# The first adaLN vectors by TensorE in quarters of the columns, and the first products in two parts along K

## The chip, the cores and the metric

The kernel runs on one core of one Trainium2 chip. The metric is the device time of the whole kernel in microseconds (us), taken as the median of several runs.

## What is computed

Two layers of a decoder trunk on one sequence of 512 tokens, 1024 features, all float32. Only the beginning of layer 0 matters here: a conditioning vector `c` gives six vectors of 1024 (shift, scale and gate of two sub-layers), the normed input is scaled and shifted by them, and one wide projection follows, of whose columns `dt`, `B` and `C` are taken first.

```
cs  = silu(c)                                   # 1024
mod = cs @ ada_w[0] + ada_b[0]                  # 1024 x 6144
sh1, sc1, g1, sh2, sc2, g2 = split(mod, 6)
h   = rms_norm(x, norm_mix_g[0]) * (1 + sc1) + sh1
z, xbc, dt_raw, q, k, v = split(h @ w_in)       # xbc: x, then B and C of 4 groups
xbc = silu(causal_depthwise_conv(xbc))          # 4 taps
dt  = softplus(dt_raw + dt_bias)
y   = ssd_chunked(x, dt, A, B, C)               # 4 groups of heads, chunks of 128 tokens
...                                             # gate by z, attention, output projection, FFN, layer 1
```

## The kernel before

Features lie on the partitions, tokens along the free axis: a product's output is 128 features by 512 tokens, one bank of PSUM. Each fp32 weight slab is split by ScalarE (ACT) and one other engine into a rounded part `hi` and a rest `lo` (`slab`), the activations likewise (`hh`, `hl` of `h`), and a product of K = 1024 is 24 matmuls: for each of 8 pieces of K `hi` and `lo` against `hh`, then 8 times `hi` against `hl` (`products`, L206, L207, L209). VectorE (DVE) makes most rests; for wdt, wbc, wx of group 0 it is GpSimd (POOL), by `SL`.

The head of the program, in the order of the code: SP loads two slabs of 1 MB for each of four column blocks of `ada_w` that the first norm needs (`ada_load`; blocks 8 and 12 are the scale, 0 and 4 the shift, 512 columns each) and `x`. `ada_wide` makes a block on DVE: one multiply and seven multiply-adds of 128 x 512 by the entries of `cs` (L159, L161), then four transposes by TensorE (PE) and a reduce. `x` is squared and scaled by its norm on ACT (`xn`), transposed by PE both as it is (`xT`, copied by ACT) and normed (`turned(xn, ...)`); ACT multiplies by the gain (`n_g`) and adds the shift (`hh`), DVE makes `hl`. Then the product of dt, then B and C of group 0 (`ssm_inputs`), whose banks go through `conv_tile` (ACT, three DVE rows that read the bank, tanh, one DVE row), the softplus of dt in a row of small DVE operations, the four products of x, then four of z.

In each of four groups, `ssm_group` then works through four chunks: `ar` is loaded from a copy of the cumulated decay in HBM, minus `acs` on POOL, minimum on DVE, exp on ACT, times `cb` on DVE, and multiplied by `xdt` on PE (`pd`). The two buffers of `ar` serve first for two tables of the attention bias (`hot`, `bv`), which PE turns into three pieces (`bv0` to `bv2`); the chunk loads can start when these are done with them.

PSUM tags `pj`, `A`, `B`, `C` have two banks each. The order of instructions on each engine is not the code's: a scheduler that simulates the engines sets it when the program is built. `tc.issue_after` holds a few rows back: the rests `hl` behind the last block of adaLN (`LATE`), the product of dt behind its last transpose (`GDT`), the loads of small vectors and of wdt behind the last adaLN load (`AFT`). adaLN columns 16 to 47 are made later, on POOL (`ada_pool`, tiles `adap`), beside the group's work.

## Time and profile before

| | |
|---|---|
| median of 3 runs | 1886.85 us (1884.89 to 1888.67) |
| the profiled execution | 1896.6 us, span 1894.8 us |
| PE busy | 1770.6 us, 93% of the span |
| DVE, ACT, POOL busy | 1150.2, 761.5, 564.4 us |
| mean granted clock of PE | 0.968 |

Busy time of PE is not work at its peak: matmuls are pipelined and a row's length holds its tail, so the distance from one start to the next is what a matmul costs in a stream. The granted clock is 1.0 at 2.4 GHz and 0.5 at 1.2 GHz; in the first 20 us the profile prints 1.00 where it has no record. Rows of the timeline merge like instructions in a row (x4) and name in brackets how long the engine stood before them and what ended that.

### The profile page before, as it was taken

To read this page: it belongs to the slowest core of one execution; us is meant where nothing else is said; L and a number is where in the kernel's file an instruction comes from. 1 tells how busy PE (TensorE), PEld (TensorE's weight loads), DVE (VectorE), ACT (ScalarE), POOL (GpSimd) and SP (SyncE) were. 2 spreads that over 40 slices of the span, in tenths; PEclk is the share of its full clock that TensorE was granted. 3 is DMA by queue.
4 is the path that set the end of the run, shared out by engine and by line. 5 is a ranking of instruction groups with operands and counts; after the bars stand their busy time and mean duration, and the time that the engine had idled before them with its cause. 6 is when DMAs were issued, how large, how long until landed. Compare 5 with 4: busy or idle time off the path is not lost.

```text
span 1894.8 us, 24381 instructions
## 1 busy us (share of the span) xinstructions
PE 1770.6 (93%) x9277; PEld 1475.4 (78%) x9277; DVE 1150.2 (61%) x2168; ACT 761.5 (40%) x1476; POOL 564.4 (30%) x486
## 2 busy tenths in 40 slices
PE   5897979999999999989999999979899899999998
PEld 3675767777788778768888888878799888888887
DVE  7859687755655565458774673386896643333336
ACT  6333333335445454245222222346775432122225
POOL 1437786412443340003000000056993400000001
PEclk8998989999999999999999999989999899999999
DMA  8354545634544543434655553242211423322223
GB/s 302 99 138 141 149 129 138 158 99 140 141 122 139 135 133 105 130 102 134 222 182 173 186 192 93 92 149 62 73 45 35 132 79 105 97 89 95 83 94 129
DMA packets 225779, 238.94 MB, mean 126 GB/s; under 512 B 11755, under 2 KB 195885, under 8 KB 225662
## 3 DMA queue, kind: packets, MB, share of 16 engines
q1 hardware_dynamic: 214525, 195.44, 34.4%
q0 software_dynamic: 11136, 41.95, 6.7%
q8 instruction: 73, 1.20, 0.3%
q14 instruction: 45, 0.36, 0.1%
HBM read 228.72 MB, written 8.64 MB: 125 GB/s over the span
## 4 chain that ended last, share of the span: by engine, by line
PE 73%; DVE 11%; DMA 6%; ACT 4%; issue 3%; POOL 2%; SPq 0%; DVEq 0%; POOLq 0%; ACTq 0%
PE fd L206 4%; PE fd L209 4%; PE fd L207 4%; PE fg L207 4%; PE fg L206 4%; PE fu L206 4%; PE fu L207 4%; PE fu L209 4%; PE fg L209 4%; PE cps L1012 2%; DMA ar<-a_dram 1%; PE s L716 1%; PE z L206 1%; PE z L207 1%; PE qq L206 1%
## 5 line engine op out<-in xcount | busy, mean ns | idle before, releaser
L248 POOL TENSOR_TENSOR n_acc<-n_acc,n_q 128x256 f32<-128x256 f32 x32 | 27.6, 864 | 545.6 <-ACT n_q L244 545.5
L194 DVE TENSOR_TENSOR wf_l<-wf_w,wf_h 128x1024 fp32r<-128x1024 f32 x88 | 106.1, 1241 | 75.7 <-ACT wf_h L193 75.7
L206 PE MATMUL fd<-uh,wd_h 128*128 128x512 f32 (+1 forms) x448 | 150.0, 351 | 0.9 <-DVE xT L591 0.9
L207 PE MATMUL fd<-uh,wd_l 128*128 128x512 f32 (+1 forms) x448 | 147.8, 346 | 0.0
L193 ACT CAST wf_h<-wf_w 128x1024 fp32r<-128x1024 f32 x88 | 87.6, 1047 | 117.5 <-PE fd L209 73.4
L207 PE MATMUL fg<-n_h,wf_l 128*128 128x512 f32 x320 | 126.0, 394 | 2.0 <-DVE wf_l L194 2.0
L206 PE MATMUL fg<-n_h,wf_h 128*128 128x512 f32 x320 | 126.2, 394 | 0.7 <-ACT wf_h L193 0.5
L206 PE MATMUL fu<-n_h,wf_h 128*128 128x512 f32 x320 | 124.8, 390 | 0.0
L207 PE MATMUL fu<-n_h,wf_l 128*128 128x512 f32 x320 | 124.7, 390 | 0.0
L990 POOL TENSOR_TENSOR cv<-cv,pr 128x256 f32<-128x256 f32 x150 | 113.7, 792 | 16.9 <-ACT pr L989 14.7
L171 POOL TENSOR_TENSOR adap<-adap 128x128 f32<-128x128 f32 (+2 forms) x96 | 104.6, 1094 | 4.7
L868 DVE TENSOR_TENSOR fs<-fs,fu 128x512 f32<-128x512 f32 x40 | 27.5, 688 | 129.1 <-PE fu L209 129.1
L591 DVE SCALAR_TENSOR_TENSOR xT<-fd,mod,xT 128x512 f32<-128x512 f32 (+1 forms) x64 | 39.1, 615 | 101.6 <-PE fd L209 101.3
L742 ACT ACTIVATE s<-s,nm 128x128 f32<-128x128 f32 x192 | 79.4, 416 | 47.4 <-DVE nm L738 38.4
L193 ACT CAST wd_h<-wd_w 128x1024 fp32r<-128x1024 f32 (+1 forms) x64 | 57.1, 940 | 103.0 <-PE fd L209 82.8
L169 POOL TENSOR_TENSOR adap<-adap,cs 128x1024 f32<-128x1024 f32 x32 | 68.2, 2131 | 88.9 <-DMA adap<-in_ada_w 88.9
L206 PEld LDWEIGHTS fd<-uh,wd_h 128*128 128x128 f32 x448 | 84.3, 188 | 13.1 <-DVE xT L591 1.3
L209 PE MATMUL fd<-ul,wd_h 128*128 128x512 f32 (+1 forms) x448 | 93.2, 346 | 0.0
L207 PEld LDWEIGHTS fd<-uh,wd_l 128*128 128x128 f32 x448 | 84.3, 188 | 11.0
L194 DVE TENSOR_TENSOR wd_l<-wd_w,wd_h 128x1024 fp32r<-128x1024 f32 (+1 forms) x64 | 67.7, 1090 | 34.9 <-ACT wd_h L193 34.8
L997 DVE SCALAR_TENSOR_TENSOR cps<-cu,taps,cps 128x256 f32<-128x256 f32 x203 | 86.9, 481 | 1.5
L161 DVE SCALAR_TENSOR_TENSOR adaa<-adaw,cs,adaa 128x512 f32<-128x512 f32 x112 | 84.8, 758 | 2.6
(418 smaller groups left out, 4913.6 us busy)
## 6 DMA issues: line engine op xcount, KB each, us to landing
adaw<-in_ada_w POOLq DMA_DIRECT2D x24, 1024.0 KB, 5.6
wf_w<-in_ffn_w_gate SPq DMA_DIRECT2D x22, 1024.0 KB
wf_w<-in_ffn_w_up SPq DMA_DIRECT2D x22, 1024.0 KB, 5.4
adap<-in_ada_w POOLq DMA_DIRECT2D x32, 512.0 KB, 5.5
...
```

The source lines that it names most:

```text
L161: V.scalar_tensor_tensor(acc, ws[k // 4][:, k % 4, :], cs[:, k:k + 1], acc, op0=ALU.mult, op1=ALU.add)
L169: G.tensor_tensor(w3, w3, cs.unsqueeze(2).broadcast_to([P, KT, P]), op=ALU.mult)
L171: G.tensor_tensor(w[:, 0:n], w[:, 0:n], w[:, n:2 * n], op=ALU.add)
L193: S.copy(hi[:, s:e], raw[:, s:e])
L194: eng.tensor_tensor(lo[:, s:e], raw[:, s:e], hi[:, s:e].bitcast(F32), op=ALU.subtract)
L206: PE.matmul(ps[:, cols], hi[:, o(k):o(k) + P], xh, start=k == 0, stop=False)
L207: PE.matmul(ps[:, cols], lo[:, o(k):o(k) + P], xh, start=False, stop=False)
L209: PE.matmul(ps[:, cols], hi[:, o(k):o(k) + P], acts[k][1][:, cols], start=False, stop=k == nk - 1)
L591: V.scalar_tensor_tensor(xT[m][:, cols], ps[:, cols], mod[l][:, go + m:go + m + 1], xT[m][:, cols], op0=ALU.mult, op1=ALU.add)
L742: S.activation(s[:, o:o + wd], s[:, o:o + wd], AF.Exp, bias=nm, accum_out=l)
L990: G.tensor_tensor(o, o, pr, op=ALU.add)
L997: V.scalar_tensor_tensor(o if t == TAPS - 1 else ps, tap(us[k], t), tapw(t, k), ps, op0=ALU.mult, op1=ALU.add)
```

## The change

The first four adaLN blocks are made on PE (`ada_rows`): `cs32` holds each piece of `cs` as a stationary operand of 32 columns, of which only the first isn't zero; eight matmuls of 128 x 32 against 128 x 512 sum into four quarters of the partitions of one bank, one quarter for k and k + 4. DVE copies the bank, and four matmuls against a column of ones add the quarters and turn the row to columns; the bias is added. The blocks are loaded in the order 8, 0, (wdt, wbc), 12, 4. `first_half(0)` makes gain and shift of the first 512 features and their `hh`, `hl`; the products of dt, B and C run over these four pieces of K (`first_products`), then `first_half(4)` and the other four. C of group 0 goes to a bank of `A`. The copies of `xT` move from ACT to DVE, the rests of wdt, wbc and wx from POOL to DVE; `LATE` and `GDT` are gone.

```diff
+    cs32 = first.tile([P, KT, 32], F32, name="cs32", bufs=1)
+    V.memset(cs32, 0.0)
+    V.tensor_copy(cs32[:, :, 0], cs)
...
-    slabs[12] = ada_load(first, 0, 12, nc.sync, 6)
-    for j0 in (0, 4):
-        slabs[j0] = ada_load(first, 0, j0, nc.sync, 6)
+    slabs[0] = ada_load(first, 0, 0, nc.sync, 6)
...
+    def ada_rows(l, j0, ws):
+        ps = bank("C", f"adar{l}_{j0}")
+        for k in range(KT):
+            g = k % 4
+            marks['ada_pe'] = PE.matmul(ps[g * 32:(g + 1) * 32, :], cs32[:, k, :], ws[k // 4][:, g, :], start=k < 4, stop=k >= 4)
+        rw = tmp.tile([P, 512], F32, tag="st_sq", name=f"adas{l}_{j0}")
+        V.tensor_copy(rw, ps)
+        pm = bank("C", f"adac{l}_{j0}", (P, 4))
+        for j in range(4):
+            PE.matmul(pm[:, j:j + 1], rw[:, j * P:(j + 1) * P], ones[:, 0:1], start=True, stop=True)
+        return V.tensor_tensor(mod[l][:, j0:j0 + 4], pm, adab[l][:, j0:j0 + 4], op=ALU.add)
...
+    def first_half(j0):
+        ada_rows(0, 8 + j0, slabs[8 + j0])
+        kk = slice(j0, j0 + 4)
+        V.scalar_tensor_tensor(g_mix0[:, kk], mod[0][:, 8 + j0:12 + j0], 1.0, nmg0[:, kk], op0=ALU.add, op1=ALU.mult)
+        ada_rows(0, j0, slabs[j0])
+        for k in range(j0, j0 + 4):
...
     for k in range(KT):
-        S.copy(xT[k], turned(xin, k, XTP[k % 2], "xtp"))
+        V.tensor_copy(xT[k], turned(xin, k, XTP[k % 2], "xtp"))
+    first_half(0)
+    wdt = slab([(win[:, 5120:5248], KT, P)], "wdt")
+    wbc0 = slab([(win[:, 4096:4096 + P], KT, P), (win[:, 4608:4608 + P], KT, P)], "wbc0")
+    for j0 in (12, 4):
+        slabs[j0] = ada_load(first, 0, j0, nc.sync, 6)
+    pre = [(wdt, grid(P, 0), bank("pj", "dt_0")), (wbc0, grid(P, 0), bank("pj", "bc0_0")),
+           (wbc0, lambda k: 1024 + k * P, bank("A", "bc0_1"))]
+
+    def first_products(ks):
+        for (hi, lo), o, ps in pre:
+            for k in ks:
+                PE.matmul(ps, hi[:, o(k):o(k) + P], h[k][0], start=k == 0, stop=False)
+                PE.matmul(ps, lo[:, o(k):o(k) + P], h[k][0], start=False, stop=False)
+            for k in ks:
+                PE.matmul(ps, hi[:, o(k):o(k) + P], h[k][1], start=False, stop=k == KT - 1)
+
+    first_products(range(0, 4))
+    first_half(4)
+    first_products(range(4, KT))
...
-            w = slab([(win[:, o:o + 256], KT, 256)], f"wx{g}_{j}", SL[2 + j] if g == 0 else V)
+            w = slab([(win[:, o:o + 256], KT, 256)], f"wx{g}_{j}")
```

Three places show how the scheduler's order moves. The first is PE where the last adaLN blocks meet dt's product, in the kernel before:

```order
L152 MATMUL ada0_0_193<-cst_72,adaa0_0_184 128x128 x4
L152 MATMUL ada0_4_209<-cst_72,adaa0_4_200 128x128 x4
L109 MATMUL cw_p_363<-cst_72,cw_r_361 128x96
L206 MATMUL dt_0_399<-n0_h0_231,wdt_h_393 128x512
L207 MATMUL dt_0_399<-n0_h0_231,wdt_l_394 128x512
```

And on PE now, between the first products' two halves (`adac0_12` turns block 12, `adar0_4` is block 4 in quarters, `xnp7` the last transposes of the normed input):

```order
L376 MATMUL bc0_1_307<-n0_l3_277,wbc0_h_291 128x512
L175 MATMUL adac0_12_355<-ones_74,adas0_12_353 128x1 x4
L170 MATMUL adar0_4_362<-adaw0_4_0_301,cs32_87 32x512 x4
L170 MATMUL adar0_4_362<-adaw0_4_1_303,cs32_87 32x512 x4
L338 MATMUL xnp7_413<-cst_72,xn0_118 128x128
L338 MATMUL xnp7_413<-cst_72,xn1_119 128x128
L338 MATMUL xnp7_413<-cst_72,xn2_120 128x128
L338 MATMUL xnp7_413<-cst_72,xn3_121 128x128
L175 MATMUL adac0_4_373<-ones_74,adas0_4_371 128x1 x4
L109 MATMUL cw_p_462<-cst_72,cw_r_460 128x96
L402 MATMUL dsk_p_474<-dsk2_471,par_470 128x16
L373 MATMUL dt_0_305<-n0_h4_386,wdt_h_282 128x512
```

All four blocks stood before the first product; now the turn of block 12 and all of block 4 stand behind its first half and before its second.

The second place is PE around the last two pieces of the attention bias, before:

```order
L209 MATMUL x0_1_1_633<-n0_l7_309,wx0_1_h_626 128x512
L558 MATMUL bv1_836<-hot_827,tab_828 16x256
L558 MATMUL bv2_839<-hot_827,tab_828 16x256
L491 MATMUL px0_0_849<-cst_72,sx1_616 128x128
L519 MATMUL pb0_0_856<-cst_72,sb16_534 128x128
L206 MATMUL z0_0_0_706<-n0_h0_231,wz0_0_h_700 128x512
```

and now (`z0_1_1` is the last of four z products, `bc1_0` the next group's B):

```order
L223 MATMUL z0_1_1_778<-n0_l7_420,wz0_1_h_771 128x512
L593 MATMUL bv2_846<-hot_834,tab_835 16x256
L526 MATMUL px0_0_856<-cst_72,sx3_697 128x128
L526 MATMUL px0_1_892<-cst_72,sx0_615 128x128
L526 MATMUL px0_1_892<-cst_72,sx1_623 128x128
L526 MATMUL px0_1_892<-cst_72,sx2_689 128x128
L526 MATMUL px0_1_892<-cst_72,sx3_697 128x128
L220 MATMUL bc1_0_1126<-n0_h0_243,wbc1_h_1120 128x512
```

`bv2`, the last reader of `hot`, moved from before the first z product to behind the last.

The third is DVE where dt's softplus begins, now; the kernel before has the same rows without those of `wx0`, which stood on POOL:

```order
L434 TENSOR_TENSOR dt_v_497<-dt_t_492,dtb_478 128x128
L436 SCALAR_TENSOR_TENSOR dt_e_498<-dt_v_497 128x128
L208 TENSOR_TENSOR wx0_0_l_560<-wx0_0_w_557,wx0_0_h_559 128x1024 x2
L477 SCALAR_TENSOR_TENSOR sb16_541<-bc0_0_306,cwh_466,sb16_541 128x511
L477 SCALAR_TENSOR_TENSOR sc20_549<-bc0_1_307,cwh_466,sc20_549 128x511
L477 SCALAR_TENSOR_TENSOR sb16_541<-bc0_0_306,cwh_466,sb16_541 128x510
L208 TENSOR_TENSOR wx0_1_l_634<-wx0_1_w_631,wx0_1_h_633 128x1024
L477 SCALAR_TENSOR_TENSOR sc20_549<-bc0_1_307,cwh_466,sc20_549 128x510
L208 TENSOR_TENSOR wx0_1_l_634<-wx0_1_w_631,wx0_1_h_633 128x1024
L438 TENSOR_SCALAR dt_w1_499<-dt_e_498 128x128
```

The four splits of wx stand among the conv rows of B and C and ahead of the rest of the softplus.

## Rows read from the trace of the kernel before

**Rows 1.** The page: the span, and the engines' shares of the chain that ended last.

```profile
span 1894.8 us, 24381 instructions
...
PE 73%; DVE 11%; DMA 6%; ACT 4%; issue 3%; POOL 2%; SPq 0%; DVEq 0%; POOLq 0%; ACTq 0%
```

**Rows 2.** Windows: the stretch in us, its length, then busy us and number of rows of PE, PE's weight loads, DVE, ACT and POOL, then PE's granted clock, the DMA engines' busy share and GB/s.

```profile
10.00:20.00 10.00, 7.03 (x28) 4.97 (x29) 7.39 (x24) 6.93 (x13) 0.00 (x0) 1.00 1.04 393
...
34.00:39.00 5.00, 1.18 (x6) 1.18 (x7) 3.69 (x5) 4.37 (x7) 3.05 (x3) 0.50 0.60 146
...
58.00:94.00 36.00, 27.89 (x117) 20.49 (x116) 29.10 (x36) 11.47 (x17) 15.00 (x11) 0.95 0.31 90
...
117.00:179.00 62.00, 47.91 (x261) 37.47 (x257) 49.25 (x59) 22.37 (x32) 36.97 (x23) 0.92 0.47 126
```

**Rows 3.** Groups of DVE rows in 0 to 40 us: line, operation, shape, count, then busy us, mean ns of one, and idle time before them.

```profile
L161 DVE SCALAR_TENSOR_TENSOR adaa<-adaw,cs,adaa 128x512 f32<-128x512 f32 x28 | 21.8, 782 | 0.5
...
L159 DVE TENSOR_SCALAR adaa<-adaw,cs 128x512 f32<-128x512 f32 x4 | 1.9, 484 | 3.4 <-DMA adaw<-in_ada_w 3.4
```

**Rows 4.** The timeline of PE in 0 to 94 us: start, length in us, line, operation, shapes, count, idle time before and what ended it.

```profile
10.79 0.43 PE L109 MATMUL pa_p<-cst,pa_r 104*128 104x104 f32 x1 [7.49 <-DMA pa_r<-in_hy_ssm_norm_g]
...
16.86 5.32 PE L330 MATMUL xtp<-cst,xin 128*128 128x128 f32 x24 [0.96 <-ACT xT L345]
...
37.82 1.11 PE L152 MATMUL ada<-cst,adaa 128*128 128x128 f32 x4 [6.58 <-DVE adaa L161]
...
38.80 0.78 PE L206 MATMUL dt<-n_h,wdt_h 128*128 128x512 f32 x1
39.37 0.63 PE L207 MATMUL dt<-n_h,wdt_l 128*128 128x512 f32 x1
39.80 0.63 PE L206 MATMUL dt<-n_h,wdt_h 128*128 128x512 f32 x1
...
50.16 1.98 PE L209 MATMUL bc<-n_l,wbc_h 128*128 128x512 f32 x8
...
58.00 0.39 PE L206 MATMUL x<-n_h,wx_h 128*128 128x512 f32 x1
...
64.31 0.50 PE L207 MATMUL x<-n_h,wx_l 128*128 128x512 f32 x1 [3.38 <-POOL wx_l L194]
...
72.34 0.47 PE L206 MATMUL x<-n_h,wx_h 128*128 128x512 f32 x1 [4.29 <-DVE sc L445]
...
93.84 0.48 PE L206 MATMUL z<-n_h,wz_h 128*128 128x512 f32 x1
```

**Rows 5.** Groups of DVE rows in 52 to 94 us, each shape apart; columns as in rows 3.

```profile
L412 DVE SCALAR_TENSOR_TENSOR dt_acc<-dt_acc,dt_w 128x128 f32<-128x128 f32 x6 | 7.9, 1316 | 0.1
L445 DVE SCALAR_TENSOR_TENSOR sx<-x,cwh,sx 128x511 f32<-128x511 f32 x4 | 2.9, 737 | 1.8 <-ACT sx L442 1.8
L449 DVE SCALAR_TENSOR_TENSOR sb<-th,sb 128x512 f32<-128x512 f32 x1 | 2.8, 2824 | 0.0
L194 DVE TENSOR_TENSOR wz_l<-wz_w,wz_h 128x1024 fp32r<-128x1024 f32 x2 | 2.4, 1217 | 0.0
...
L449 DVE SCALAR_TENSOR_TENSOR sx<-th,sx 128x512 f32<-128x512 f32 x3 | 2.1, 693 | 1.5 <-ACT th L448 1.5
```

**Rows 6.** The timeline of PE in 136 to 139 us: `pd` with 64 columns of weights, `po` and `pst` with 128; columns as in rows 4.

```profile
136.05 1.09 PE L503 MATMUL pd<-ar,xdt 128*64 128x128 f32 x16
137.07 1.16 PE L515 MATMUL po<-sc,prev 128*128 128x128 f32 x8
138.07 1.02 PE L525 MATMUL pst<-xde,btok 128*128 128x512 f32 x2
```

**Rows 7.** The timeline of ACT in 21 to 39 us: scaling of x, gain, shift and the splits of wdt and wbc.

```profile
21.14 4.27 ACT L319 ACTIVATE xn<-xin,n_y 128x1024 f32<-128x1024 f32 x4
...
26.25 4.75 ACT L337 ACTIVATE n_g<-xnp,g_mix 128x512 f32<-128x512 f32 x8
...
32.80 2.56 ACT L340 ACTIVATE n_h<-n_g,mod 128x512 fp32r<-128x512 f32 x4
35.27 1.12 ACT L193 CAST wdt_h<-wdt_w 128x512 fp32r<-128x512 f32 x2
36.30 2.08 ACT L193 CAST wbc_h<-wbc_w 128x1024 fp32r<-128x1024 f32 x2
```

**Rows 8.** Single rows of the timelines of DVE and POOL in 52 to 65 us.

```profile
52.53 0.29 DVE L402 TENSOR_TENSOR dt_v<-dt_t,dtb 128x128 f32<-128x128 f32 x1 [0.91 <-PE dt_t L391]
...
58.74 1.95 POOL L169 TENSOR_TENSOR adap<-adap,cs 128x1024 f32<-128x1024 f32 x1
...
61.87 2.39 POOL L194 TENSOR_TENSOR wx_l<-wx_w,wx_h 128x1024 fp32r<-128x1024 f32 x1
```

**Rows 9.** Single rows of the timelines of SP, DVE and PE in 93 to 179 us: the first load of a chunk's `ar`, the product with `cb`, the first `pd`, and the first z product of group 1.

```profile
93.75 0.37 SPq L485 DMA_DIRECT2D ar<-a_dram  x1
...
102.52 1.23 DVE L499 TENSOR_TENSOR ar<-ar,cb 128x1024 f32<-128x1024 f32 x1 [0.53 <-ACT ar L488]
...
116.59 1.09 PE L503 MATMUL pd<-ar,xdt 128*64 128x128 f32 x16
...
178.72 0.77 PE L206 MATMUL z<-n_h,wz_h 128*128 128x512 f32 x1 [3.08 <-DVE sx L445]
```

More of the change, by code (lines that the diff above doesn't have):

```diff
@@ L320, in trunk_kernel @@
     g_mix0 = const.tile([P, KT], F32, name="g_mix0")
-    for j0 in (8, 12, 0, 4):
-        last_ada = ada_wide(tmp, "st_sq", 0, j0, slabs[j0])
-        if j0 >= 8:
-            k = slice(j0 - 8, j0 - 4)
-            V.scalar_tensor_tensor(g_mix0[:, k], mod[0][:, j0:j0 + 4], 1.0, nmg0[:, k], op0=ALU.add, op1=ALU.mult)
     def turned(src, k, tag, name):
@@ L344, in trunk_kernel @@
-    for k in range(KT):
-        S.copy(xT[k], turned(xin, k, XTP[k % 2], "xtp"))
+    def first_half(j0):
[4 more added lines that the diff above has]
+        for k in range(j0, j0 + 4):
+            t = first.tile([P, T], F32, tag="xg", name=f"n0_g{k}", bufs=6)
+            S.mul(t, turned(xn, k, "BABABABB"[k], "xnp"), g_mix0[:, k:k + 1])
+            hh = hpool.tile([P, T], F32R, tag="hh", name=f"n0_h{k}")
+            hl = hpool.tile([P, T], F32R, tag="hl", name=f"n0_l{k}")
+            S.activation(hh, t, AF.Identity, bias=mod[0][:, k:k + 1])
+            V.scalar_tensor_tensor(hl, t, mod[0][:, k:k + 1], hh.bitcast(F32), op0=ALU.add, op1=ALU.subtract)
+            h.append((hh, hl))
@@ L381, in trunk_kernel @@
     ssm = ctx_s.enter_context(tc.tile_pool(name="ssm", bufs=2))
-    w = slab([(win[:, 5120:5248], KT, P)], "wdt", SL[0])
     after_ada.__exit__(None, None, None)
-    with tc.issue_after(marks["adat"].ins) if GDT else nullcontext():
-        (dps,) = products(w, [grid(P, 0)], h, "dt")
+    dps = pre[0][2]
     draw = ssm.tile([HEADS, T], F32, tag="xe", name="draw", bufs=3)
@@ L452, in ssm_inputs @@
     def ssm_inputs(g):
-        w = slab([(win[:, 4096 + g * P:4096 + (g + 1) * P], KT, P), (win[:, 4608 + g * P:4608 + (g + 1) * P], KT, P)],
-                 f"wbc{g}", SL[1] if g == 0 else V)
-        pb, pc = products(w, [grid(P, 0), lambda k: 1024 + k * P], h, f"bc{g}")
+        if g == 0:
+            pb, pc = pre[1][2], pre[2][2]
+        else:
+            w = slab([(win[:, 4096 + g * P:4096 + (g + 1) * P], KT, P), (win[:, 4608 + g * P:4608 + (g + 1) * P], KT, P)],
+                     f"wbc{g}")
+            pb, pc = products(w, [grid(P, 0), lambda k: 1024 + k * P], h, f"bc{g}")
         bt = conv_tile(pb, 16 + g, "sb", 2)
```

10 lines of the change are left out of this document (1 added, 9 removed).

## The prediction

> **What bounds the kernel now.** I read the page first. The chain that ended last is TensorE for 73% of its time [rows 1], so a change that only frees VectorE (DVE) or GpSimd (POOL) is worth nothing unless TensorE (PE) was standing still for them. The windows show where it was [rows 2]: in 34 to 39 us PE is busy 1.18 of 5 us, in 58 to 94 us 27.89 of 36, in 117 to 179 us 47.91 of 62. DMA moves 393 GB/s in 10 to 20 us with all its engines busy, so loads there run at their ceiling. What the change can win lies before 94 us; what it can lose as well as win lies in 117 to 179.
>
> The rows say why PE stood. Each column block of adaLN costs DVE one multiply and seven multiply-adds; for four blocks that is 21.8 + 1.9 = 23.7 us [rows 3]. The last block's transposes wait 6.58 us for it, and dt's first matmul follows at 38.80 [rows 4]. It starts at the half clock: matmuls 0.43 us apart, granted clock 0.50 in the window before it [rows 2, 4], after an idle stretch; at full clock eight take 1.98 us with the tail of the last, 0.227 apart. The first x product starts at 58.00, stops 3.38 us for a POOL split of wx, the second starts after 4.29 us for DVE, and z starts at 93.84: 35.84 us for four products of 24 matmuls, 4 x 5.45 = 21.8 us of PE work. In that stretch DVE rows are stretched: six dt_acc rows take 7.9 us, an sb row 2.82 where three rows of the same form take 0.69 each [rows 5].
>
> **The change, part by part.** It is all in the first 58 us of code, but the scheduler moves rows up to the first FFN.
>
> *DVE loses* the 23.7 us and four reduces. *It gains* eight copies of xT and four of a bank (nearest row, an evacuation by conv or z, some 0.6 us each) and the splits of wdt, wbc and wx, which POOL leaves. None of that is a gain by itself; it counts by what PE waits for.
>
> *PE gains* 32 fp32 matmuls of 32 x 512. A full-width fp32 matmul of 512 columns is two records and 1.02 us with the tail of the last (pst, [rows 6]); a pass of 512 columns being 0.227, I take a record as two passes, 0.43 us at full clock. Whether four quarters run at once, no row shows. The nearest are the half-width pd rows: 16 records in 1.09 us, where 8 full-width po records of as many columns take 1.16, so two halves do run together. I take four together: 2 x 0.43 = 0.86 us per half block at full clock, 1.7 at half; the other end is one after another, 3.4 and 6.8. Switching between widths costs little by the same rows: pd to po is 1.02 us from start to start, eight pairs of 0.11 us are 0.87, leaving 0.15 per visit. The Trainium skill, TensorEngine Tiling (Array Packing), Key Properties, says that changing the tiling mode drains TensorE; this speaks against weaving quarters among transposes, and by it some twelve changes would add an estimated 1.8 us, mostly where PE waits anyway. The trace agrees with a price of that size for halves.
>
> *The chain to the first pair of slabs.* Quarters of block 8 stand behind pa_p in PE's order, which ends at 11.22 [rows 4]; 3.4 us at half clock, to 14.6. The 32 transposes of x then take 0.22 each as before (24 in 5.32). In DVE's new order five of the copies of xT and one of the bank stand before the end of the Newton steps, of which I put 1.5 us on the chain (0 to 3.6: all six at 0.6), so the scaling of x starts at 22.6, not 21.14, and its four rows (4.27) end at 26.9 [rows 7]. ACT then does wdt and wbc (1.12 + 2.08), four n_g (half of 4.75) and the first n_h (0.64): 33.1. Slabs don't bind: four blocks, x, wdt and wbc are 12 MB at 393 GB/s, 31 us, with block 4 last; it is used at 43. SP issues wdt and wbc ahead of blocks 12 and 4 and the small loads behind; the one that ACT waits for, nega, stands with the table load under the first half's matmuls.
>
> *First products, first half*: 36 matmuls. PE has done little for some 9 us before them, so I take the half clock for nine (3.9 us, as at 38.80), then 27 x 0.227 = 6.1: to 43.1. *Between the halves* the new order has the column turn of block 12 (some 0.6), the gain on DVE (0.4), four n_g on ACT (2.4) and one n_h (0.64); block 4's quarters, copy and turn fit beside them: 47.2. *Second half*: 36 x 0.227 = 8.2, to 55.4. Before, this point was 58.00: **2.6 us won**. Ends: no half clock 2 us more; all of the first half at the half clock, 5.4 us less.
>
> *The x stage.* From the dt bank on, DVE's order sets it, since pj has two banks and a product waits until conv has read the bank it takes. From dt's first row to the conv that frees z's bank, DVE's new order holds four wx splits and two of wz at 1.22 (7.3), 15 conv rows at 0.74 (11.1), four closing rows at 0.69 (2.8) and 16 dt rows at 0.29, one of them, the reciprocal, 0.7 longer (5.3): 26.5 us [rows 5, 8]. Before, wx was POOL's (2.39 us each), but the dt_acc and sb rows were longer than such rows are alone by 7.9 - 6 x 0.29 + 2.82 - 0.69 = 8.3 us. Now POOL has only the adap rows, some 10 us (its 15.00 in 58 to 94 less three wx splits, and the first multiply), and they fall on the wx splits. Not held up at all, these cost 0 more; each of four held up by one POOL multiply of 1.95, 7.8; I take 3, since the bank-reading conv rows between them (0.74, no longer than elsewhere) leave POOL time to run. Started at 56.2 (dt's bank is done some 0.8 us before the last B and C matmuls; then copy and transposes), z starts at 56.2 + 26.5 + 3 = 85.7. Before, 93.84: **8.1 us won in all**. The Trainium skill, SBUF — State Buffer, section SBUF: two separate sides, says that a DVE row with two SBUF inputs and a GpSimd row exclude each other for the whole instruction. The trace agrees in that rows with two SBUF inputs are the long ones (2.82) and bank-reading ones are not (0.74); by the rule alone the splits' move to DVE would cost up to the 7.8 and leave 3.3 us.
>
> *Behind z.* Work is the same, order is not. One row moves against the change: the bias matmuls that free the buffer ar stood before z (bv2 just before 93.84) and now stand after its last product, at 85.7 + 21.8 = 107.5. So the first load of ar goes out 13.75 us later than at 93.75 [rows 9]. In the kernel before, chunk 0's product was ready at 103.75 (102.52 + 1.23) and used at 116.59: 12.8 us of slack, which this eats; the two bc1 products (2 x 5.45 us) now stand in front of pd and cover the load's way. I put that at 0, between 7 us won (half of the 14 us that PE idles in 117 to 179) and 13.75 lost. From there to the end TensorE is the chain, and the shift stays.
>
> **Sum**: 8.1 us. The profiled execution took 1896.6 us (span 1894.8 [rows 1]), which would become 1888.5; it is 9.75 above the median of the runs, 1886.85, and I take the same shift for these: 1878.75, rounded **1879.0 us**.
>
> **The rivals.**
> A. The stage after z fills up. DVE and POOL enter it with less behind them; if half of PE's idle 14 us goes, 7 us more: 1872. For: DVE is busy 49.25 of 62 there and z of the next group waits 3.08 us for it [rows 2, 9]. Against: the conv rows still stand behind the y rows in the new order.
> B. The port. All four splits are held up, and PE waits for wx as it did 3.38 us before: 4.8 us of the gain go, 1883.5, and with the whole first half at half clock nothing is left: up to 1889. Against: POOL has half the work it had in that stretch.
> C. Slower: the late load of ar. If chunk 0 and 1 aren't covered by bc1 because their rows crowd DVE among the conv rows, the whole 13.75 us come back: 1886.85 - 8.1 + 13.75 = 1892.5. It decides once PE stands over 8 us more than before in front of pd0 or the x products of group 1. For: DVE's order puts the second chunk's minimum in front of group 1's conv, so conv waits for that load too. Against: 12.8 us of slack in the trace.
> D. The quarters don't overlap: 6.8 or 13.7 us a block instead of 1.7 or 3.4. Block 8 then delays the transposes and, through the copies of xT, the scaling by some 8 us, block 4 the second half by 5: first products end near 68, z starts at 98: 1891. Against: the pd rows.
>
> **Chances.** Forecast (4 to 12 us won) 0.45, A 0.22, B 0.16, C 0.12, D 0.05. About 0.2% (3.8 us) is what a measurement of this kernel can tell from no change. Faster is the forecast and A, 0.67; same is B and a little of D, 0.17; slower is C and the rest of D, 0.16. The range leaves out a tenth at each end: below, A with a first half at full clock throughout, under 1870, and more of the idle time gone; above, C at 1892.5.
>
> **What would show it.** Right: quarter matmuls in fours starting together; dt's first matmul near 33 and a gap of some 4 us between the halves; first x product near 56, z near 86; wx splits on DVE at 1.2 to 3 us; first ar load near 107, pd by 121. Wrong: z before 80 or after 92; PE idle in front of pd; quarter records 0.43 us apart one by one; the shift at the second group's z far from 8 us, which would mean that the scheduler's new order in the SSD stage, not the start, decides.

## The result: slower by 0.45%, where a gain was forecast

The changed kernel takes 1893.72 us (median of 20 runs, 1889.09 to 1902.85), the kernel before 1886.4 beside it (20 runs, 1878.17 to 1896.07); the ratio is 1.0045, interval 1.0032 to 1.0059, so 6 to 11 us slower. Forecast were 1879.0 and "faster".

The two profiled executions hide this: 1895.62 us now, 1896.6 before. One execution of either kernel can lie 9 or 10 us from its median, and in the two pairs of profiles most of the difference lies behind the first 430 us. The time of an execution goes with its mean granted clock: over 35 executions of the kernel before (clock 0.965 to 0.977) the correlation is -0.84, some 1.5 us for each 0.001. The median clock of the changed kernel is 0.9715 and that of the kernel before 0.972, so the loss does not lie there. The marks within the first 430 us repeat better. Both kernels were profiled a second time (e17 and e18 below); the table has both, starts in us, and for `ys_s` (the last product of the SSD stage) the end.

| mark | before | again (e17) | changed | again (e18) | mean difference |
|---|---|---|---|---|---|
| first x product | 58.0 | 58.8 | 58.6 | 59.3 | +0.6 |
| first z product, group 0 | 93.8 | 92.3 | 88.4 | 89.2 | -4.3 |
| first load of `ar` | 93.8 | 92.2 | 113.5 | 114.2 | +20.8 |
| first `pd` | 116.6 | 115.1 | 130.9 | 131.6 | +15.4 |
| first z product, group 1 | 178.7 | 177.4 | 175.5 | 174.7 | -3.0 |
| group 2 | 255.9 | 253.6 | 256.6 | 255.5 | +1.3 |
| group 3 | 340.1 | 338.0 | 348.7 | 347.0 | +8.8 |
| last `ys_s` | 420.3 | 416.6 | 427.7 | 426.0 | +8.4 |

So z of group 0 starts 4.3 us earlier, and 12.7 us are lost between there and the end of the SSD stage; 11.8 of them fall between the z products of group 1 (-3.0) and of group 3 (+8.8). The sum, 8.4, is the difference of the medians (7.3) and of the ratio (8.5) within what a median is uncertain by.

### The profile page after: what moved, and what is told of

Read it like the earlier page. It is cut to its first block, busy times and chain, and to the rows that moved or that the text cites. A ratio compares the mean times of both kernels' runs of the same rounds, so it can differ in the third digit from the quotient of the medians.

```text
span 1893.9 us, 24510 instructions
## 1 busy us (share of the span) xinstructions
PE 1776.7 (94%) x9357; PEld 1475.5 (78%) x9357; DVE 1141.9 (60%) x2154; ACT 758.0 (40%) x1468; POOL 551.3 (29%) x478
## 4 chain that ended last, share of the span: by engine, by line
PE 75%; DVE 10%; DMA 6%; POOL 3%; issue 3%; ACT 2%; SPq 1%; DVEq 0%; POOLq 0%; ACTq 0%
PE fd L220 4%; PE fd L223 4%; PE fd L221 4%; PE fg L221 4%; PE fg L220 4%; PE fu L220 4%; PE fu L221 4%; PE fu L223 4%; PE fg L223 4%; DMA ar<-a_dram 2%; PE s L751 2%; PE cps L1047 2%; PE qq L220 1%; PE qq L221 1%; PE qq L223 1%
## 5 line engine op out<-in xcount | busy, mean ns | idle before, releaser
L185 POOL TENSOR_TENSOR adap<-adap 128x512 f32<-128x512 f32 (+2 forms) x96 | 106.2, 1113 | 4.0
L777 ACT ACTIVATE s<-s,nm 128x128 f32<-128x128 f32 x192 | 79.4, 415 | 43.8 <-DVE nm L773 37.7
L1024 ACT ACTIVATE pr<-cu,taps 128x256 f32<-128x256 f32 x150 | 72.9, 506 | 27.2 <-POOL cv L1025 26.9
```

Source lines behind the costliest of these rows:

```text
L185: G.tensor_tensor(w[:, 0:n], w[:, 0:n], w[:, n:2 * n], op=ALU.add)
L777: S.activation(s[:, o:o + wd], s[:, o:o + wd], AF.Exp, bias=nm, accum_out=l)
L1024: S.mul(pr, tap(us[k], t), tapw(t, k))
```

## The profile after

The page's span and the engines' shares of the chain that ended last answer to [rows 1]: still TensorE, and POOL's share is 3% where it was 2%.

```profile
span 1893.9 us, 24510 instructions
...
PE 75%; DVE 10%; DMA 6%; POOL 3%; issue 3%; ACT 2%; SPq 1%; DVEq 0%; POOLq 0%; ACTq 0%
```

The windows that answer to [rows 2], in the same columns, with two more: 94 to 428 us, and the stretch around the first two `pd`.

```profile
34.00:39.00 5.00, 5.00 (x28) 3.38 (x21) 2.06 (x4) 1.81 (x3) 0.00 (x0) 0.93 0.49 163
58.00:94.00 36.00, 31.92 (x132) 25.51 (x132) 33.85 (x51) 15.94 (x23) 11.18 (x8) 0.91 0.31 91
94.00:428.00 334.00, 290.50 (x1507) 229.10 (x1506) 241.27 (x280) 112.87 (x163) 191.30 (x131) 0.93 0.48 133
117.00:179.00 62.00, 49.66 (x257) 38.62 (x256) 49.60 (x61) 23.16 (x32) 38.73 (x25) 0.88 0.50 137
130.50:137.00 6.50, 6.07 (x36) 4.32 (x36) 6.50 (x8) 4.04 (x7) 1.04 (x1) 0.50 0.36 67
```

TensorE is busy 5.00 of 5 us in 34 to 39, where it was busy 1.18. Yet the first x product starts no earlier. TensorE's timeline in 33 to 60 us (answering to [rows 4]) says why:

```profile
33.20 1.78 PE L170 MATMUL adar<-adaw,cs 128*32 128x512 f32 x8
34.91 0.50 PE L373 MATMUL dt<-n_h,wdt_h 128*128 128x512 f32 x1
...
42.78 1.07 PE L376 MATMUL bc<-n_l,wbc_h 128*128 128x512 f32 x4
43.69 0.95 PE L175 MATMUL adac<-ones,adas 128*128 128x1 f32 x8
44.57 1.92 PE L170 MATMUL adar<-adaw,cs 128*32 128x512 f32 x16
46.42 0.66 PE L338 MATMUL xnp<-cst,xn 128*128 128x128 f32 x4
47.30 1.05 PE L175 MATMUL adac<-ones,adas 128*128 128x1 f32 x8 [0.23 <-DVE adas L172]
48.22 0.28 PE L109 MATMUL cw_p<-cst,cw_r 96*128 96x96 f32 x1
48.61 0.39 PE L402 MATMUL dsk_p<-dsk,par 2*128 2x16 f32 x2
49.43 0.50 PE L373 MATMUL dt<-n_h,wdt_h 128*128 128x512 f32 x1 [0.42 <-ACT n_h L355]
...
56.83 1.07 PE L376 MATMUL bc<-n_l,wbc_h 128*128 128x512 f32 x4
...
58.60 0.49 PE L220 MATMUL x<-n_h,wx_h 128*128 128x512 f32 x1 [0.34 <-ACT wx_h L207]
```

Between the halves (43.69 to 49.43) TensorE stands for 0.23 + 0.42 us; the rest is its own rows: columns turned, quarters of block 4, transposes, small vectors. What it got earlier it pays with work that was DVE's or lay beside DVE's.

In the x stage DVE's groups in 58 to 89 us answer to [rows 5]. The six dt_acc rows take 1.7 us instead of 7.9; the four wx rests, now DVE's, 8.1:

```profile
L208 DVE TENSOR_TENSOR wx_l<-wx_w,wx_h 128x1024 fp32r<-128x1024 f32 x4 | 8.1, 2038 | 0.0
...
L208 DVE TENSOR_TENSOR wz_l<-wz_w,wz_h 128x1024 fp32r<-128x1024 f32 x2 | 2.4, 1221 | 0.0
...
L444 DVE SCALAR_TENSOR_TENSOR dt_acc<-dt_acc,dt_w 128x128 f32<-128x128 f32 x6 | 1.7, 289 | 0.1
```

Behind z, single rows of SP, POOL, DVE and PE answer to [rows 9]:

```profile
113.45 0.37 SPq L520 DMA_DIRECT2D ar<-a_dram  x1
...
118.82 1.90 POOL L521 TENSOR_TENSOR ar<-ar,acs 128x1024 f32<-128x1024 f32 x1
...
120.75 0.69 DVE L522 TENSOR_SCALAR ar<-ar 128x1024 f32<-128x1024 f32 x1 [2.83 <-POOL ar L521]
...
127.57 1.52 DVE L522 TENSOR_SCALAR ar<-ar 128x1024 f32<-128x1024 f32 x1 [5.27 <-POOL ar L521]
129.67 1.21 DVE L534 TENSOR_TENSOR ar<-ar,cb 128x1024 f32<-128x1024 f32 x1
...
130.93 1.97 PE L538 MATMUL pd<-ar,xdt 128*64 128x128 f32 x16 [4.22 <-DVE ar L534]
...
175.49 0.77 PE L220 MATMUL z<-n_h,wz_h 128*128 128x512 f32 x1 [5.09 <-DVE sx L477]
```

The load goes out at 113.45 instead of 93.75. In DVE's order the second chunk's minimum stands in front of the first chunk's product with `cb`, so DVE waits 5.27 us for the second load before it makes what TensorE needs for the first. TensorE then stands 4.22 us, and the next 6.5 us run at a granted clock of 0.50: `pd` takes 1.97 us, where it took 1.09 [rows 6]. The larger part shows later. The first `pd` comes 15 us later than before, and the marks then slip in the next two groups; the waits that the profile names for PE in 94 to 430 us add up to 43.1 and 44.5 us in the two profiles now, and to 34.9 and 32.9 in those of the kernel before. The longest stop, rows of DVE, POOL and PE in 259 to 276 us:

```profile
259.25 8.20 DVE L570 SCALAR_TENSOR_TENSOR y<-sx,dsk,y 128x512 f32<-128x512 f32 x4
...
268.04 4.50 DVE L208 TENSOR_TENSOR wz_l<-wz_w,wz_h 128x1024 fp32r<-128x1024 f32 x2
...
274.76 0.28 DVE L533 TENSOR_TENSOR cb<-pb,cst 128x128 f32<-128x128 f32 x1
...
260.20 1.30 POOL L185 TENSOR_TENSOR adap<-adap 128x512 f32<-128x512 f32 x1
261.45 1.90 POOL L521 TENSOR_TENSOR ar<-ar,acs 128x1024 f32<-128x1024 f32 x1
263.31 1.26 POOL L571 TENSOR_TENSOR y<-y,z 128x512 f32<-128x512 f32 x1
...
275.10 0.47 PE L554 MATMUL pb<-cst,sb 128*128 128x128 f32 x1 [12.38 <-DVE cb L533]
```

Four y rows take 8.20 us while POOL goes from one row to the next, and 2.74 in group 2 (364.36), where POOL has little; two wz rests take 4.50 where two took 2.4. TensorE stands 12.38 us for the small cb row behind them. Such a stop is no mark of the change, though. In the kernel before four y rows take 7.02 us there and TensorE stops 9.06 us:

```profile
257.11 7.02 DVE L535 SCALAR_TENSOR_TENSOR y<-sx,dsk,y 128x512 f32<-128x512 f32 x4
...
271.10 0.76 PE L206 MATMUL z<-n_h,wz_h 128*128 128x512 f32 x1 [9.06 <-DVE sx L445]
```

And e1 below, 13 us faster than the changed kernel, has it as long:

```profile
252.61 8.88 DVE L570 SCALAR_TENSOR_TENSOR y<-sx,dsk,y 128x512 f32<-128x512 f32 x4
...
269.12 0.48 PE L554 MATMUL pb<-cst,sb 128*128 128x128 f32 x1 [12.25 <-DVE cb L533]
```

So the rows show how DVE and POOL hold TensorE up in all these kernels; of the 12.7 us they show some 3. A stop that the kernel before does not have is one of 7.89 us in front of an x product at 327.02, for DVE's sc (3.96 us in e1). The view of tile `y` (shortest, median and longest row in ns), in the changed kernel, shows which rows are stretched:

```profile
L570 DVE SCALAR_TENSOR_TENSOR y<-sx,dsk,y x16: 740/750/5206, 167.1 to 416.3; 128x512 f32<-128x512 f32 x16
...
L551 DVE TENSOR_TENSOR y<-po,ef x12: 677/684/692, 147.3 to 412.8; 128x512 f32<-128x512 f32 x12
```

Both are 128 x 512. The first reads both operands from SBUF and is up to seven times as long beside POOL; the second reads a bank, and none of its 12 rows is stretched. Rows with one SBUF operand can be stretched too: the minimum at 127.57 took 1.52 us with a POOL row beside it (1.04 us from 127.50), the one at 120.75 took 0.69 with none.

## The experiments

Time is the median, ratio that to the runs of the kernel before on the same chip, with its interval. z is the first z product of group 0, ys the end of the last `ys_s`, in the one profiled execution. The letters in the expectations: **S**, the late `ar` load loses what the start won; **N** and **N'**, the later groups lose it whatever the load does; **P** and **P'**, DVE rows stretched beside POOL decide; **O** and **B**, the order of rows alone decides; **F**, the shorter start has a worth of its own.

| | time | ratio | z | ys |
|---|---|---|---|---|
| e1 changed, bias in a buffer of its own | 1880.76 | 0.9958 (0.9939 to 0.9977) | 88.0 | 417.6 |
| e2 before, first blocks on TensorE | 1888.39 | 1.0001 (0.9979 to 1.0024) | 92.6 | 422.2 |
| e3 changed, first blocks on DVE | 1898.15 | 1.0057 (1.0037 to 1.0078) | 89.9 | 427.6 |
| e4 changed, rests on POOL | 1890.27 | 1.0012 (0.999 to 1.0035) | 94.7 | 415.1 |
| e5 changed, bias ahead of z | 1887.59 | 0.9997 (0.9974 to 1.002) | 94.5 | 427.2 |
| e6 before, bias in a buffer of its own | 1896.15 | 1.0047 (1.003 to 1.0065) | 93.8 | 433.8 |
| e7 before, bias behind z | 1899.75 | 1.0064 (1.004 to 1.0088) | 90.1 | 429.7 |
| e8 e1, quarters among the first half | 1880.44 | 0.997 (0.9953 to 0.9988) | 89.7 | 414.7 |
| e9 e1, POOL's jobs in the attention stage | 1919.68 | 1.0191 (1.0163 to 1.0218) | 85.3 | 388.8 |
| e10 e1, y times z on DVE | 1881.52 | 0.9977 (0.9955 to 1.0) | 91.0 | 421.9 |
| e11 e1, B's transpose first | 1886.34 | 1.0006 (0.9989 to 1.0023) | 88.6 | 418.5 |
| e12 before, POOL's jobs in the attention stage | 1924.9 | 1.0205 (1.0177 to 1.0233) | 85.0 | 391.9 |
| e13 e1, POOL's jobs on TensorE | 1884.58 | 0.9988 (0.9967 to 1.001) | 85.4 | 408.9 |
| e14 changed, POOL's jobs on TensorE | 1881.05 | 0.9968 (0.9948 to 0.9987) | 85.5 | 411.8 |
| e15 before, POOL's jobs on TensorE | 1871.71 | 0.9927 (0.9899 to 0.9955) | 83.9 | 405.9 |
| e16 e15, first blocks on TensorE too | 1871.83 | 0.9907 (0.9877 to 0.9938) | 85.3 | 408.6 |
| e17 before, again | 1884.83 | 0.9981 (0.996 to 1.0002) | 92.3 | 416.6 |
| e18 changed, again | 1894.68 | 1.0034 (1.0011 to 1.0057) | 89.2 | 426.0 |

### The late load of ar: e1, e7, e5, e6

**e1**: `hot` and `bv` leave the buffers of `ar` for that of `y1`, which is first written after them.

```diff
-    hot = ssm.tile([P, HPG, P], F32, tag="ar", name="hot").rearrange("p h l -> p (h l)")[0:33, 0:LTOT]
+    hb = ssm.tile([P, 4, T], F32, tag="y1", name="hb", bufs=1).rearrange("p t l -> p (t l)")
+    hot = hb[0:33, 0:LTOT]
...
-    bv = ssm.tile([P, HPG, P], F32, tag="ar", name="bv").rearrange("p h l -> p (h l)")[0:16, 0:LTOT]
+    bv = hb[0:16, 1024:1024 + LTOT]
```

> The changed kernel, with the two tables of the attention bias in the buffer of y1 and no longer in the two of ar, so that the chunk loads need not wait for the bias matmuls behind z. Theory S (the late ar load and the order that hangs on it lose what the start won): the first load goes out well before z ends, the 4.22 us in front of pd0 go, with them the half clock there (some 3 us), and the time is 1886 to 1889. Theory N (the late load is covered; the later groups' order loses it alone): pd0's wait goes but the end of the last group (ys_s, 427.7 us) stays within 2 us and the time is 1892 to 1895. Theory P (DVE and POOL share a port, DVE has too much work in the x stage): no change of the total, 1893.

The timelines of SP, DVE and PE in e1:

```profile
98.31 0.99 SPq L520 DMA_DIRECT2D ar<-a_dram  x2
...
109.40 1.22 DVE L534 TENSOR_TENSOR ar<-ar,cb 128x1024 f32<-128x1024 f32 x1
...
118.57 1.09 PE L538 MATMUL pd<-ar,xdt 128*64 128x128 f32 x16
```

13.0 us faster than the changed kernel, more than S foretold: the start and z are as in the changed kernel, `pd` comes 12.4 us earlier, and ys 10.1. z of group 1 is no earlier (175.9, was 175.5); the gain appears at group 2 (250.7, was 256.6) and 3 (338.8, was 348.7). So what the edit wins is won in the later groups. Not all of it need be the load's: the order of TensorE's rows in the groups changed with it, the end of `ys_s` (417.6) is hardly earlier than that of the kernel before (418.4 in the mean of two) though the time is 8 us less than before, and the median clock is 0.975 where the changed kernel has 0.9715.

**e7** is the converse: before, with only the bias matmuls moved behind z.

```diff
+                marks['prod'] = PE.matmul(ps[:, cols], hi[:, o(k):o(k) + P], acts[k][1][:, cols], start=False, stop=k == nk - 1)
...
+        with tc.issue_after(marks['prod'].ins):
             PE.matmul(bp, tab[:, g * 16:(g + 1) * 16], hot[:, OB[g]:OB[g] + n], start=True, stop=True)
```

> The kernel before with one thing added: the bias matmuls are issued behind the last z product of group 0, so that the first ar load goes out at about 117 instead of 93.75. z stays at 93.84. Theory S: the late load alone makes the kernel slower by 10 to 15 us, 1896 to 1902, with pd of group 0, chunk 0 near 135 and the last ys_s product at 430 or later. Theory N (the load is covered by the products of group 1): 1886 to 1889.

SP and PE in e7:

```profile
119.15 0.37 SPq L485 DMA_DIRECT2D ar<-a_dram  x1
...
133.83 1.09 PE L503 MATMUL pd<-ar,xdt 128*64 128x128 f32 x16
```

As S said: 12 us by the ratio, though z was even earlier (90.1). The edit delays only the bias matmuls, but the scheduler wove the groups anew around them: z of group 1 comes at 167.0 (before 178.7), of group 2 at 264.5 (255.9). So a late load with its order costs about as much in either kernel; apart from the order it was not measured.

**e5** puts the bias code ahead of `ssm_inputs(0)` and the z products behind its last matmul.

```diff
+            with tc.issue_after(marks['bv'].ins) if g == 0 else nullcontext():
+                pz = products(w, [grid(256, 0), grid(256, 1)], h, f"z{g}_{j}")
```

> The changed kernel with the bias tables in the ar buffers as they were, but the bias matmuls put ahead of the first z product by a dependence (their code moved up, z issued behind them). Theory S: what costs is the time at which the ar buffers come free; the first ar load goes out by 90, pd of group 0, chunk 0 by 119 instead of 130.9, and the time is that of the kernel with a buffer of its own, 1879 to 1884. Theory B (the gain with a buffer of its own is that of a luckier order in the later groups, whatever the bias does): nothing that can be foretold, 1885 to 1895.

Only half of S: the load goes out at 94.56 and `pd` comes at 113.9, but z starts at 94.5, 6.0 us later than in the changed kernel. The last x product ends at nearly the same time (87.4, in the changed kernel 87.8); the transposes of acs and the bias matmuls, which now stand in front of z, wait for DVE. With the bias ahead of z, as before, the changed kernel takes the time of before: 0.9997. In this order its new start is worth nothing that can be measured. The end of `ys_s`, 427.2, is that of the changed kernel all the same, though the time is 9 us less by the ratio: what comes behind that mark differs by several us from kernel to kernel too, so the mark is not the time.

**e6** is e1's edit on the kernel before.

> The kernel before, with the bias tables in the buffer of y1 as in the first experiment. There the first ar load already went out at 93.75, and its chunk had 12.8 us of slack. Theory S: no more than 2 us won, 1884 to 1888. Theory B (the buffer of its own is worth as much in any kernel): 13 us won as in the changed kernel, 1871 to 1876.

Neither: 9 us slower than before, with the start unchanged and `pd` 3 us earlier. Its waits of PE in 58 to 430 us (place, releaser, us in total, times, longest) and those of the changed kernel:

```profile
PE pb L519 <- DVE cb L498: 29.8, 3, 13.6
```

```profile
PE pb L554 <- DVE cb L533: 12.9, 2, 12.4
```

The scheduler wove the chunks otherwise, and three of them now meet POOL as in the rows at 259 us. Order by itself is worth some 9 us here, so e1's 13 us and e7's 12 can hold some of that too. What speaks for the load is the whole series. Where POOL's jobs stay in the groups, the three kernels whose first load goes out at 113 us or later (the changed one, e3, e7) take 1.0034 to 1.0064; of the eight with a first load at 86 to 102 us (e1, e2, e4, e5, e6, e8, e10, e11) all but e6 take 0.9958 to 1.0012.

### Which part of the change won at z: e2, e3, e4, e8

**e2**: before, `ada_rows` instead of `ada_wide` for the four first blocks. **e3**: the changed kernel with `ada_wide`. **e4**: the changed kernel with the rests of wdt, wbc and wx on POOL.

```diff
-        last_ada = ada_wide(tmp, "st_sq", 0, j0, slabs[j0])
+        last_ada = ada_rows(0, j0, slabs[j0])
```

```diff
-        ada_rows(0, 8 + j0, slabs[8 + j0])
+        ada_wide(tmp, "st_sq", 0, 8 + j0, slabs[8 + j0])
```

```diff
+            w = slab([(win[:, o:o + 256], KT, 256)], f"wx{g}_{j}", SL[2 + j] if g == 0 else V)
```

> The kernel before with the four adaLN blocks made by TensorE in quarters, nothing else (one buffer less for n_g, for room): loads in the old order, undivided products, the rests of wdt, wbc, wx on POOL, copies of xT on ACT. TensorE's order in the groups is nearly that of before, with the bias matmuls ahead of z. Theory S: what the start wins stays; DVE is free of 23.7 us, dt's first matmul at 33 to 36 instead of 38.80, z at 87 to 91 instead of 93.84, and the end of the groups (ys_s, 420.3 us before) as much earlier: 1880 to 1884. Theory N' (any change at the start is eaten in the groups): z earlier but ys_s end at 419 to 421, time 1885 to 1888. Theory P: z near 93 since the x stage is bound by POOL and DVE as before, 1886.

> The changed kernel with the adaLN blocks on DVE again (one multiply, seven multiply-adds): only the two parts along K, the load order, DVE's rests and copies are left of the change. DVE has 23.7 us more before the second half. The bias matmuls stand behind z, as in the changed kernel. Theory S: dt starts no earlier than 40, the second half ends at 62 to 66, z at 92 to 96, and the late ar load comes on top: 1897 to 1903. Theory N or P: the start counts for little, 1892 to 1896.

> The changed kernel with the rests of wdt, wbc of group 0 and wx of group 0 on POOL again. In its order the bias matmuls stand ahead of z and the first ar load behind them, as before the change. Theory S: the first ar load by 95, no wait in front of pd0, z at 87 to 92, time 1884 to 1888. Theory P (the splits on DVE beside POOL cost the x stage): z earlier than in the changed kernel (88.44), by up to 3 us, time 1886 to 1890. Theory N: z where it was, ys_s end at 425 to 429, time 1891 to 1895.

e2 wins nothing that can be told from before, nearest to P. e3 keeps most of the lead at z (89.9, earlier than S said) with adaLN on DVE, and has the late load and S's time. e4's order has the bias matmuls ahead of z again: z at 94.7, no late load, and a time above S's range that cannot be told from before. P's gain at z from the rests does not show in e4 beside e5: z is at 94.7 and 94.5, with the rests on POOL and on DVE. Much of the lead hangs on which small rows of TensorE stand ahead of z. In before the transposes of acs and the bias matmuls do (83.6 to 84.2, 86.0 to 86.8, 92.7 to 93.7: 2.4 us), in the changed kernel they come behind the first z product; and e7, the old start with the bias behind z, has z at 90.1, 3 us earlier than before's mean. So some 2.4 to 3 of the 4.3 us are rows put off, not work saved.

**e8** puts blocks 12 and 4 among the first half in e1.

```diff
+    first_products(range(0, 4), pre[:1])
+    vectors(4)
+    with tc.issue_after(marks['ada_pe'].ins):
+        first_products(range(0, 4), pre[1:])
```

> The first experiment (bias tables in the buffer of y1) with the quarters of blocks 12 and 4 taken among the first half of the first products instead of behind it: dt's first four pieces, then the two blocks, then B and C. In the changed kernel block 4's quarters stood at 44.57, though its last load had landed at about 36, and the second half began at 49.43, 5.6 us after the end of the first. Theory S: the gap between the halves shrinks to 2 to 3 us, the first x product starts at 55 to 57 instead of 58.8, z as much earlier, and the time is 1877 to 1880. Rival (DVE sets the x stage from dt's first row on): z at 88 as before, 1880 to 1882.

PE in e8:

```profile
40.61 1.06 PE L170 MATMUL adar<-adaw,cs 128*32 128x512 f32 x8
...
46.72 0.95 PE L175 MATMUL adac<-ones,adas 128*128 128x1 f32 x8
48.08 1.03 PE L338 MATMUL xnp<-cst,xn 128*128 128x128 f32 x8
...
49.45 0.50 PE L377 MATMUL dt<-n_h,wdt_h 128*128 128x512 f32 x1
```

The quarters went early, the second half did not (49.45): the turn of their columns was put behind B and C. The first x product came at 59.5. There was hardly an idle gap to close. z at 89.7 and the time are the rival's.

### POOL's jobs: e9 to e16

**e9** and **e12** drop `ada_some(ssm, 2, 8)` from e1 and from before, and take six or four jobs a pair of heads; **e10** replaces G by V for y times z; **e11** exchanges the two products of `pb`.

```diff
-            ada_some(ssm, 2, 8)
...
-        ada_some(att, 1, 3)
+        ada_some(att, 1, 6 if hp < 2 else 4)
```

> The first experiment (bias tables in the buffer of y1) with POOL's adaLN jobs taken out of the x stage and of the groups and all made in the attention stage (6 each beside the first two pairs of heads, 4 beside the others, instead of 16 in the groups and 3 a pair). Theory P' (the stops of TensorE in the groups are DVE rows with two operands in SBUF that stand still while POOL works: four y rows took 8.2 us at 259 to 267 in the changed kernel, of which 3 are needed): wx rests on DVE near 1.25 us each instead of 5.13 for two, z at 84 to 86 instead of 88.0, DVE's rows in the groups at their shortest, the 12.2 us stop in front of pb halved, the last ys_s product 10 to 15 us earlier than 417.6; of this some comes back in the attention stage: 1868 to 1878. Rival O (DVE and TensorE stop for the order of their rows, POOL's work is hidden): ys_s end within 4 us of 417.6, time 1878 to 1886.

> The kernel before with POOL's adaLN jobs moved out of the x stage and the groups as in e9. Theory P': the six dt_acc rows (7.9 us for 1.7) and the sb row (2.82 for 0.69) shrink, z at 88 to 90 instead of 93.84, the last ys_s product 10 to 15 us earlier than 420.3, time 1873 to 1882. Rival O: 1882 to 1890.

> The first experiment with the product of y and z of groups 0 to 2 on DVE instead of POOL (12 rows of 128 x 512; for group 3 it is there already). Theory P': 12 x 0.7 = 8.4 us more for DVE, but these rows take as much of POOL's time beside DVE's y rows away; the stop of 12.2 us in front of pb becomes 8 to 10, 1877 to 1881. Rival O: DVE is what TensorE waits for, 4 to 8 us slower, 1885 to 1889.

> The first experiment with the transpose of B put ahead of the product of B and C in the bank pb, so that TensorE no longer stands in front of it until DVE has read the product (cb); that wait was the longest of the groups: 12.2 us in the first experiment, 12.4 in the changed kernel, 29.8 in all in the kernel before with a buffer of its own. Theory O (the order of rows decides; this one row blocks TensorE's queue): the wait goes and 5 to 12 us with it, 1869 to 1876. Theory P': the wait turns into one for the conv rows (sx) at the same place, since DVE's rows are what is late: 1878 to 1883.

Without the jobs the SSD stage ends 27 to 29 us earlier in both (388.8 and 391.9), far more than P' said; the stages behind give back more than twice that, so the totals, far outside the range of P', say nothing of it. z comes at 85.3 and 85.0: the lead of the new start is gone. e10 is half a us above the range of P', with ys 4.3 us later than in e1. e11 takes away the wait for cb, and TensorE stands for x products instead (15.4 us for DVE's sx): that is the turn that P' foretold, but the time is above its range, 9 us slower than e1 by the ratios.

**e13**, **e14**, **e15** make columns 16 to 31 by `ada_rows` on e1, the changed kernel and before; **e16** adds e2's edit to e15. (The stationary operand is now cut from a row of `cs` and zeros, in e13 and e14 for the first four blocks too, and `tab` lies in the buffer of `hot`.)

```diff
-            ada_some(ssm, 2, 8)
+            for j0 in (16 + 8 * g, 20 + 8 * g):
+                ada_rows(0, j0, ada_load(ssm, 0, j0, nc.sync, 1))
```

> The first experiment (bias tables in the buffer of y1) with columns 16 to 31 of adaLN, which POOL made in 16 jobs beside the x stage and the groups, made by TensorE in quarters as well, four blocks, two behind group 0 and two behind group 1; the attention stage keeps its 16 jobs on POOL. (The stationary operand is 32 columns out of a row of cs and zeros, and a selection column takes the first row of each quarter.) Theory P': without POOL's jobs DVE's rows run at their shortest, as with all jobs moved (ys_s end at 388.8 instead of 417.6), four blocks cost TensorE some 4 x 3 us, ys_s ends at 395 to 405 and the time is 1862 to 1872. Rival O: POOL's rows were hidden and only their moving changed the order; ys_s end within 5 us of 417.6, 1877 to 1890.

> The changed kernel (bias tables in the ar buffers, bias matmuls behind z) with columns 16 to 31 of adaLN on TensorE as in e13. Theory S: the late ar load still costs some 10 us against e13, 1872 to 1884. Theory P' alone (the late load only mattered because POOL and DVE were crowded): within 3 us of e13.

> The kernel before with columns 16 to 31 of adaLN on TensorE as in e13; the first four blocks stay on DVE, products undivided. With all jobs moved (e12) z came at 85.0, as early as with the change and no jobs (e9: 85.3). Theory P': what the change won at z was DVE rows that no longer met POOL's jobs; without the jobs the start of before is as good, so this kernel is within 4 us of e13, 1864 to 1874. Theory F (the shorter start is worth its 5 us by itself): 5 to 8 us slower than e13.

> The kernel of e15 (before, with columns 16 to 31 on TensorE) with the first four blocks on TensorE in quarters too; loads, undivided products, the rests on POOL and the copies of xT on ACT as before. e15 took 1871.7 us, with z at 83.9. Theory P' (without POOL's jobs the start has nothing left to win, because loads and TensorE's own work bound it): z at 83 to 85, time 1869 to 1875. Theory F (DVE's 23.7 us of adaLN still hold the start): z 2 to 4 us earlier, 1865 to 1869.

The window 94 to 428 us of e15, beside that of the changed kernel above: POOL 109 us instead of 191, DVE 218 instead of 241, and TensorE does 137 more rows in it. The second line is the kernel before, of which e15 is an edit.

```profile
94.00:428.00 334.00, 305.07 (x1644) 238.26 (x1644) 218.25 (x322) 123.90 (x199) 109.35 (x64) 0.97 0.50 141
...
94.00:428.00 334.00, 299.01 (x1555) 237.97 (x1555) 236.69 (x313) 116.56 (x168) 187.98 (x131) 0.94 0.50 137
```

DVE's groups in 58 to 86 us of e13: the same wx rests on the same engine, without POOL's jobs beside them, take 4.8 us, not 8.1.

```profile
L210 DVE TENSOR_TENSOR wx_l<-wx_w,wx_h 128x1024 fp32r<-128x1024 f32 x4 | 4.8, 1214 | 0.0
```

e15 and e16 are the best kernels of this study, 14 and 18 us faster than before by the ratio; both beat both kernels, and both have the old loads and undivided products. Part of that goes with the clock: its median is 0.978 and 0.979, beside 0.971 and 0.970 of the kernel before in the same series. e16 cannot be told from e15, so in this order DVE's 23.7 us of adaLN hold nothing up: F falls. e14 is no slower than e13: without the jobs the late load (`pd` at 128.0, in e13 at 116.1) costs nothing that can be told, which suggests that it was dear because POOL and DVE were full. It is not more than that, since the order changed as well, and e13 missed what P' said for it (ys 395 to 405, 1862 to 1872): it has ys at 408.9, earlier than e1's 417.6, and yet is no faster than e1 (0.9988 and 0.9958). The same edit won 13 us on the changed kernel (e14) and 14 on the kernel before (e15). Why it won nothing on e1, and why e13 and e14 are some 10 us slower than e15, is open.

**e17** and **e18** are the two kernels again.

> The kernel before, unchanged, for a second profile. If the marks of one profiled execution can be read to a microsecond in the groups (z at 93.84, last ys_s product at 420.3), both come back within 1.5 us and the two executions differ behind the groups alone; otherwise the comparison of single profiles above has to be read with that spread.

> The changed kernel, unchanged, for a second profile: z at 88.4, the last ys_s product at 427.7, within 1.5 us if the groups' marks repeat; 1893 to 1895 in the median.

z repeats within 1.5 us; ys within 1.8 us for the changed kernel, but only within 3.7 for before, more than was expected. A difference of less than 4 us at ys, from one profile each, says nothing, nor does a ratio within 0.002 of 1: e17, the same kernel, has 0.9981.

## Why the prediction was wrong, step by step

**Quarters.** Right: 16 records in 1.92 us and 8 in 1.06, forecast 1.7 and 0.86 without the tail of the last; they overlap, rival D is out. From block 4's quarters to the transposes behind them is 1.85 us; four times 0.43 is 1.72, so 0.13 us are left for the change of width, near the 0.15 that the prediction read from halves. The Trainium skill (TensorEngine Tiling (Array Packing), Key Properties) says that changing the tiling mode drains TensorE; more than that 0.13 us a drain did not cost here.

**To the first half.** The first n_h was done near 32.5 (forecast 33.1), dt started at 34.91, the half was done at 43.8 (43.1). The half clock did not fall on the products (granted clock 1.00 in 34.9 to 39 us) but on the transposes and the quarters of block 12 in front of dt (0.50 in 32.0 to 33.2, 0.56 in 33.2 to 34.9): eight quarters took 1.78 us there, 1.06 at 30.31. Transposes stood among the products besides.

**First products.** Wrong by the whole term: forecast 2.6 us won, with the second half done at 55.4. It was done at 57.9, before at 58.2, and the first x product came 0.6 us later in the mean of two profiles. dt started 1.8 us later than forecast, and the step took the time between the halves, 4.1 us, as a wait beside which other rows fit. It was TensorE's own work, 5.7 us with 0.65 idle.

**x stage.** Right in size: 58.30 (dt's first row) to 88.44 is 30.1 us, forecast 29.5. The 3 us put on POOL's jobs were 3.3 (8.1 against 4.8 for the wx rests, e13), so rival B's 7.8 was too much. The Trainium skill (SBUF — State Buffer, SBUF: two separate sides) has a DVE row with two SBUF operands and a GpSimd row exclude each other; rows of that kind are the long ones here (5206 against 740 ns), and rows that read a bank are not. A row with one SBUF operand was long too (1.52 against 0.69 us, at 127.57). But the stretch of before that this was set against, up to 93.84, held 2.4 us of small TensorE rows which the new order only puts behind z, so the lead of 4.3 us is at best half a gain. Without POOL's jobs there is no lead at all (e9 85.3, e12 85.0, though e12 still has bias matmuls ahead of z), which points to DVE rows that no longer met POOL as what was won beyond the order.

**Behind z, put at 0.** The step that failed. I saw the load 13.75 us later, set 12.8 us of slack and the two bc1 products against it, and let them cancel. Measured: the load 20.8 us later, since z came 2.7 us later than forecast and the four z products with the rows among them took 25.0 us and not 21.8, and 12.7 us lost by ys. Slack of one chunk was the wrong cover: the whole row of chunks moved, and the loss came where the prediction did not look, between the z products of groups 1 and 3. How much of it is the load and how much the order that the scheduler wove around it is open (e5, e6, e7). The sign of being wrong that the prediction named last did come: the shift at the second group's z was 3.0 us, not 8. **Rival C** had the price (13.75; e1 13.0, e7 12), but the wrong sign to look for: TensorE stood 4.22 us in front of `pd`, not 8. That its 1892.5 lies near the measured time is in part luck, since 8.1 us won became 4.3. It had 0.12 of the chances, too little for a load moved by 13.75 us with DVE and POOL busy in the groups.

**Sum.** With the measured terms: 1886.4 - 4.3 + 12.7 = 1894.8, measured 1893.72. The sum takes what lies behind ys as unchanged, which e1 and e5 do not bear out for every kernel.
